# A two-layer hybrid encoder step in split fp32: squares of norms written to PSUM, adaLN reductions and two down tiles in another order

## The chip, the cores and the metric

The kernel runs on one core of a Trainium2 chip. The metric is the time of one execution on the device, in microseconds; lower is better. Before the change the median of three runs is 2359.96 us (2359.71 to 2361.61). The names used below: TensorE (PE) multiplies matrices, VectorE (DVE) and ScalarE (ACT) work element by element, GpSimd (POOL) too, and SyncE (SP) starts most DMAs.

## The reference, cut to what matters

Two groups of tokens share the weights: 512 prompt tokens and 32 sample tokens, 544 columns in all. Each of two layers has a half-step feed-forward block, a mixing block and a second half-step feed-forward block. Each block stands between two RMS norms, and each has a shift, a scale and a gate that come from a conditioning vector (adaLN).

```python
def rmsnorm(x, g):
    xf = x.astype(F32)
    r = lax.rsqrt(jnp.mean(xf * xf, axis=-1, keepdims=True) + EPS)
    return (xf * r).astype(x.dtype) * g

def swiglu(h, wg, wu, wd):
    return (jax.nn.silu(h @ wg) * (h @ wu)) @ wd
...
        mod = (jax.nn.silu(c) @ lp["w_mod"] + lp["b_mod"]).reshape(b_, N_SUB, 3, D_MODEL)
        shift, scale, gate = mod[:, :, 0, None], mod[:, :, 1, None], mod[:, :, 2, None]

        def pre(x_, j):
            return rmsnorm(x_, lp["norm_pre"][j]) * (1.0 + scale[:, j]) + shift[:, j]

        def post(x_, y_, j, w):
            return x_ + w * gate[:, j] * rmsnorm(y_, lp["norm_post"][j])

        y = swiglu(pre(x, 0), lp["ffn_w_gate"][0], lp["ffn_w_up"][0], lp["ffn_w_down"][0])
        x = post(x, y, 0, 0.5)
        y, st = token_mix(pre(x, 1), lp, prev, ssd_block)
        x = post(x, y, 1, 1.0)
        y = swiglu(pre(x, 2), lp["ffn_w_gate"][1], lp["ffn_w_up"][1], lp["ffn_w_down"][1])
        x = post(x, y, 2, 0.5)
```

D_MODEL is 1024 and D_FF is 2816. The adaLN vectors are a product of a vector of 1024 with a matrix of 1024 x 9216 in each layer.

## The kernel before, in words

The model's rows lie on partitions in 8 blocks of 128 (KD), and the tokens in two chunks c = 0 and 1 of 272 columns (CA). The whole trunk keeps fp32: a weight tile is loaded to `raw`, ScalarE copies it to a rounded `hi`, GpSimd subtracts to get `lo` (`wload`), and activations are split in the same way into `hh` and `hl`. `gemm` therefore does three matmuls for each block k (lines 276 to 278): hi by high, hi by low, lo by high.

**Feed-forward block** (`ffn`). The 22 blocks of D_FF are worked in three parts, 0 to 8, 8 to 15 and 15 to 22 (`THIRDS`). Within a part, `up(f, c, W)` makes a gate and an up product of 24 matmuls each, `g` and `u`, then Silu on ScalarE, the product on VectorE (line 421), its rounded copy on ScalarE (line 422) and the remainder on VectorE (line 423). After the gate/up tiles of a part come its down tiles, for m = 0 to 7 chunk 0 and then chunk 1, each over the 7 or 8 blocks of that part; VectorE copies the result to `Y` (line 466) or adds it (line 468). In the last part each finished `Y[m]` also goes into the sum of squares of the norm that follows (`accs[c].add(y)`).

**Norms.** An `Acc` sums squares: the first one is written to the sum itself, and for each other one `sq` (line 285) has ScalarE write the square to one of two `sq` buffers in SBUF (line 287), and VectorE, or for the blocks k in PACC GpSimd, adds it (line 321). Then `rstd` multiplies the sum by a matrix of ones on TensorE (line 296), which adds over partitions, and `finish` takes the root by Ln and Exp. `chain` returns the list of these steps for one chunk: the norm behind a block (`yacc`), `post_k` for each of 8 blocks (X is updated, lines 363 and 365, and its square goes into the next norm's sum, `acc`), the next norm and `pre_k`, which writes `hh` (line 334) and `hl` (line 335) for the next block. `weave` puts a chain's steps between the units of TensorE's work: chunk 0's chain beside the down tiles of chunk 1 in the last part, chunk 1's chain beside the first five gate/up tiles of the next block. The out-projection of the mixing block (`full`, `rest`) has the same sums.

**PSUM.** `gps6` hands out banks in turn: three `g`, two `pv` and one `tp`; while steps are woven in, three `g` and the `tp`, because the steps use the two `pv` banks for their own products (`t` in `post_k` and `pre_k`).

**adaLN.** Layer 0's first vectors are made ahead; all others come from a `Fill`: one job is a DMA of 256 KB of the adaLN weights (`mw`, three buffers, on SyncE's queue beside the weight tiles) and two VectorE reductions (line 177, `junk`), one for each token group, each followed by a short read of its sum. `fill.step(us, tail)` first issues the reductions of the jobs loaded so far, behind the instruction `tail`, and then loads so many more that all jobs would be spread over FILL_US. There is a step behind each gate/up tile and behind each down tile that isn't in the last part. Layer 0's first feed-forward block has 112 jobs, its second 96, layer 1's first 48, its second none.

What sets the order: TensorE's order is the order in which the code calls `gemm`; the instructions of VectorE and ScalarE are placed by the framework's scheduler, which holds those given with `tc.issue_after` behind the instruction named. DMAs of weights stand on one queue, and a DMA whose buffer isn't free yet holds those behind it.

Of the kernel before, what the change touches and what calls it, by code (L numbers as in the profile page):

```python
# [10 lines left out]
F32 = mybir.dt.float32  # L11
# [3 lines left out]
ALU = mybir.AluOpType  # L15
# [5 lines left out]
KD = 8  # L21
# [3 lines left out]
CA = 272  # L25
NF = 22

NHEAD = 5
FILL_US = 290

NPART = 4

# [35 lines left out]
def trunk_kernel(ctx: ExitStack, tc: tile.TileContext, a):  # L68
# [16 lines left out]
    X = [slot(f"x{k}") for k in range(KD)]  # L85
# [196 lines left out]
    SEG = (((0, CA, 0),), ((CA, SP, 0), (SP, T, 1)))  # L282


    def sq(ap):
        q = tp_.tile([128, CA], F32, tag="sq", bufs=2, name="sq")
        S.activation(q, ap, AF.Square)
        return q

# [21 lines left out]
    class Acc:  # L311
# [1 line left out]
            self.a = None  # L313
            self.tag = tag

        def add(self, ap, eng=None):
            if self.a is None:
                self.a = tp_.tile([128, CA], F32, tag=self.tag, bufs=2, name=self.tag)
                S.activation(self.a, ap, AF.Square)
            else:  # L320
                (eng or V).tensor_tensor(self.a, self.a, sq(ap), ALU.add)  # L321


    def pre_k(l, j, c, r, ks):
# [20 lines left out]
    def chain(l, j, c, Y, acc, nxt, free):  # L345
        st = {}
        xacc, pacc = Acc("acc"), Acc("acc")

        def first():
            st["r"] = rstd([acc.a], 1.0, False, bool(nxt) or c == 0)  # L350

        def post_k(k):
            if c and not nxt:
                t = tmp()
                e = G if k in FIN else V
                e.tensor_tensor(t, Y[k][:, CS[c]], st["r"], ALU.mult)
                e.tensor_tensor(X[k][:, CS[c]], X[k][:, CS[c]], t, ALU.add)
                SY.dma_start(a["o_y"][:, k, CS[c]], X[k][:, CS[c]])
                return
            t = ppv()[:, :CA]  # L360
            for (c0, c1, tok) in SEG[c]:
                o0 = c0 - c * CA
                V.scalar_tensor_tensor(t[:, o0:o0 + c1 - c0], Y[k][:, c0:c1], gpc[l][:, j, k, tok:tok + 1],
                                       st["r"][:, o0:o0 + c1 - c0], ALU.mult, ALU.mult)
            V.tensor_tensor(X[k][:, CS[c]], X[k][:, CS[c]], t, ALU.add)
            if nxt:
                if k in PACC:
                    pacc.add(X[k][:, CS[c]], G)
                else:
                    xacc.add(X[k][:, CS[c]])  # L370
            else:
                SY.dma_start(a["o_y"][:, k, CS[c]], X[k][:, CS[c]])
            if free:
                done(Y[k])

        def second():
            st["r"] = rstd([t.a for t in (xacc, pacc) if t.a is not None], 1.0, c == 1 and nxt[1] != 1, True)

        ops = [first] + [lambda k=k: post_k(k) for k in range(KD)]
        if nxt:  # L380
            ops += [second] + [lambda k=k: pre_k(*nxt, c, st["r"], [k]) for k in range(KD)]
        return ops
# [14 lines left out]
    def ffn(l, i, fill, pend, nxt, W0=(), first=(), behind=None):  # L397
# [3 lines left out]
        for ti, (f0, f1) in enumerate(THIRDS):  # L401
# [29 lines left out]
            if f == 0:  # L431
# [16 lines left out]
                    tail = up(f, 1, Ws[f] if n < 3 else load(f))  # L448
                    fill.step(5.6, tail)
                f = NHEAD  # L450
            while f < f1:
                W = load(f)
                fill.step(5.6, up(f, 0, W))
                fill.step(5.6, up(f, 1, W))
                f += 1
            nk = f1 - f0
            last = ti == 2
            if ti == 0:
# [2 lines left out]
            def down(m, c, W):  # L461
                ps = gps6()
                gemm(ps, W, range(nk), act, c)
                y = Y[m][:, CS[c]]
                if ti == 0:
                    tail = V.tensor_copy(y, ps[:, :CA])
                else:
                    tail = V.tensor_tensor(y, y, ps[:, :CA], ALU.add)
                if last:
                    accs[c].add(y)  # L470
                    if c and not nxt:
                        post_scale(l, j, m, y)
                else:
                    fill.step(0.35 * nk, tail)
# [2 lines left out]
                return wload(a["wd"][l, i, m][:, f0:f1, :], nk * 128, 2 if last else 1)  # L477

            if not last:
                for m in range(KD):  # L480
                    W = wdl(m)
                    down(m, 0, W)
                    down(m, 1, W)
            else:
                fill.flush()
                lnexp()
                Ws = []
                for m in range(KD):
                    Ws.append(wdl(m))
                    down(m, 0, Ws[m])  # L490
                units = []
                for n in range(KD):
                    m = (n + 2) % KD
                    units.append(lambda n=n, m=m: down(m, 1, Ws[m] if n < 6 else wdl(m)))
                weave(units, chain(l, j, 0, Y, accs[0], nxt, False), CUT_DN)
# [33 lines left out]
    def mix(l, pend, nxt):  # L529
# [551 lines left out]
        def full(m, c, W):  # L1081
            ps = gps6()
            gemm(ps, W, range(7), HX, c, stop=False)
            gemm(ps, W2, [m], HX[7:], c, start=False)
            S.activation(Y[m][:, CS[c]], ps[:, :CA], AF.Copy)
            accs[c].add(ps[:, :CA])

        def rest(m):
            ps = gps6()
            gemm(ps, W2, [m], HX[7:], 0)  # L1090
            y = Y[m][:, CS[0]]
            V.tensor_tensor(y, y, ps[:, :CA], ALU.add)
            accs[0].add(y)

        def wo(m):
            return wload(a["wo1"][l, m], 7 * 128, 2)
# [194 lines left out]
```

## Time and profile before

| what | value |
| --- | --- |
| median of three runs | 2359.96 us (2359.71 to 2361.61) |
| the profiled execution's own time | 2355.58 us |
| span of its trace | 2353.8 us |
| mean granted clock of TensorE | 0.977 |
| TensorE busy | 2224.8 us, 95% of the span |
| VectorE busy | 1465.6 us, 62% |
| ScalarE busy | 892.7 us, 38% |
| GpSimd busy | 1031.2 us, 44% |

All durations that follow come from the one profiled execution, whose time is 4.4 us below the median. The span is the time from the first to the last instruction of the trace. A row that names a line tells the line of the kernel before, and in the helpers `gemm`, `sq` and `Acc.add` one line serves many places; they are told apart by the names of the tiles and by the time. In a timeline row the bracket at the end holds the time for which the engine stood idle before the instruction, and what ended that.

### The profile page before, as it was taken

How to read it: one execution, taken by the hardware profiler on the slowest of the kernel's cores; microseconds unless marked ns; L12 is line 12 of the kernel's file. 1: busy time of each engine (PE TensorE's matmuls, PEld its weight loads, DVE VectorE, ACT ScalarE, POOL GpSimd, SP SyncE). 2: the span in 40 equal slices, each digit the busy share in tenths (PEclk: the TensorE clock that was granted, in tenths of full speed). 3: DMA queues.
4: the chain of work that ended last, by engine and by line, in shares of the span. 5: the costliest groups of instructions: out<-in, count | busy, mean ns of one | idle time of the engine just before them, and what ended most of it. 6: DMA issues, size and time to landing. Idle time of an engine off the chain costs nothing.

```text
span 2353.8 us, 44051 instructions
## 1 busy us (share of the span) xinstructions
PE 2224.8 (95%) x17554; PEld 2163.4 (92%) x17554; DVE 1465.6 (62%) x3281; ACT 892.7 (38%) x1796; POOL 1031.2 (44%) x689
## 2 busy tenths in 40 slices
PE   6999999988899899999989999999789999999997
PEld 5989999988888899999989999998788799999997
DVE  5798999687766779687575544447876754111114
ACT  4322222445555631222264122235555554322223
POOL 3544344553434554344355434434643444533432
PEclk9999999998999999999999999999899999999999
DMA  7454555322222345555434444332232222322222
GB/s 274 157 175 166 171 187 170 110 66 78 94 74 74 108 157 185 158 177 162 128 108 130 143 125 133 119 91 70 95 94 71 94 87 90 117 90 80 91 84 70
DMA packets 104017, 285.62 MB, mean 121 GB/s; under 512 B 12001, under 2 KB 14689, under 8 KB 103809
## 3 DMA queue, kind: packets, MB, share of 16 engines
q1 hardware_dynamic: 102146, 277.72, 36.9%
q0 software_dynamic: 1664, 5.07, 0.6%
q8 instruction: 138, 2.26, 0.4%
q14 instruction: 69, 0.57, 0.1%
HBM read 275.45 MB, written 7.30 MB: 120 GB/s over the span
## 4 chain that ended last, share of the span: by engine, by line
PE 70%; DVE 15%; issue 5%; DMA 4%; ACT 3%; POOL 3%; SPq 0%; POOLq 0%; DVEq 0%; ACTq 0%
PE g L277 12%; PE g L276 12%; PE g L278 12%; PE pv L277 6%; PE pv L278 6%; PE pv L276 6%; PE tp L276 3%; PE tp L277 3%; PE tp L278 3%; DVE junk L177 3%; DMA raw<-in_wgu 3%; POOL lo L266 2%; DVE u L564 1%; DVE acc L321 1%; PE pv L957 1%
## 5 line engine op out<-in xcount | busy, mean ns | idle before, releaser
L266 POOL TENSOR_TENSOR lo<-raw,hi 128x1024 fp32r<-128x1024 f32 (+4 forms) x498 | 918.7, 1856 | 1154.1 <-ACT hi L262 996.9
L277 PE MATMUL g<-hl,hi 128*128 128x272 f32 (+1 forms) x2402 | 699.5, 292 | 7.3 <-DVE hl L335 4.2
L276 PE MATMUL g<-hh,hi 128*128 128x272 f32 x2402 | 700.3, 293 | 6.4 <-ACT hh L334 4.9
L278 PE MATMUL g<-hh,lo 128*128 128x272 f32 (+1 forms) x2402 | 699.3, 292 | 0.0
L262 ACT ACTIVATE hi<-raw 128x1024 fp32r<-128x1024 f32 (+3 forms) x454 | 360.2, 810 | 662.4 <-PE g L277 241.0
L277 PEld LDWEIGHTS g<-hl,hi 128*128 128x128 f32 (+1 forms) x2402 | 457.3, 191 | 10.4 <-DVE hl L335 5.3
L276 PEld LDWEIGHTS g<-hh,hi 128*128 128x128 f32 x2402 | 456.5, 190 | 9.9 <-ACT hh L334 6.6
L278 PEld LDWEIGHTS g<-hh,lo 128*128 128x128 f32 (+1 forms) x2402 | 455.9, 190 | 0.7
L177 DVE CUSTOM_DVE_ANT_0 junk<-mw,csb,modr 128x512 bf16<-128x512 f32 x256 | 310.5, 1213 | 6.8 <-DMA mw<-in_wmod 1.0
L177 DVE CUSTOM_DVE_ANT_0 junk<-mw,csb 128x512 bf16<-128x512 f32 x256 | 275.3, 1075 | 7.0 <-DMA mw<-in_wmod 1.6
L278 PE MATMUL pv<-hh,lo 128*128 128x272 f32 (+1 forms) x916 | 264.0, 288 | 2.5 <-POOL lo L266 2.5
L276 PE MATMUL pv<-hh,hi 128*128 128x272 f32 (+1 forms) x916 | 264.1, 288 | 0.6 <-DVE hl L335 0.6
L277 PE MATMUL pv<-hl,hi 128*128 128x272 f32 (+1 forms) x916 | 264.4, 289 | 0.0
L276 PE MATMUL g<-u,hi 128*128 128x272 f32 x732 | 211.9, 290 | 6.7 <-ACT u L422 6.7
L277 PE MATMUL g<-u,hi 128*128 128x272 f32 x732 | 211.6, 289 | 0.2
L278 PE MATMUL g<-u,lo 128*128 128x272 f32 x732 | 211.0, 288 | 0.0
L421 DVE TENSOR_TENSOR g<-sg,g 128x272 f32<-128x272 f32 x123 | 54.5, 443 | 211.2 <-PE g L278 203.0
L278 PEld LDWEIGHTS pv<-hh,lo 128*128 128x128 f32 (+1 forms) x916 | 171.8, 188 | 2.9 <-POOL lo L266 2.9
L276 PEld LDWEIGHTS pv<-hh,hi 128*128 128x128 f32 (+1 forms) x916 | 172.2, 188 | 1.0 <-DVE hl L335 0.8
L277 PEld LDWEIGHTS pv<-hl,hi 128*128 128x128 f32 (+1 forms) x916 | 171.9, 188 | 0.0
L276 PE MATMUL tp<-hh,hi 128*128 128x272 f32 x554 | 162.9, 294 | 1.7 <-ACT hh L334 1.7
L277 PE MATMUL tp<-hl,hi 128*128 128x272 f32 x554 | 161.6, 292 | 0.0
(342 smaller groups left out, 3978.5 us busy)
## 6 DMA issues: line engine op xcount, KB each, us to landing
raw<-in_wgu SPq DMA_DIRECT2D x192, 512.0 KB, 3.6
mw<-in_wmod SPq DMA_DIRECT2D x256, 256.0 KB, 3.1
raw<-in_wd SPq DMA_DIRECT2D x72, 448.0 KB, 3.5
raw<-in_win SPq DMA_DIRECT2D x48, 512.0 KB, 3.5
raw<-in_wd SPq DMA_DIRECT2D x32, 512.0 KB, 3.7
raw<-in_wo SPq DMA_DIRECT2D x22, 448.0 KB, 3.2
u<-in_wmod SPq DMA_DIRECT2D x32, 256.0 KB, 5.3
kc<-in_kc SPq DMA_DIRECT2D x8, 512.0 KB, 4.5
```

Source lines behind the costliest of these rows:

```text
L177: V.tensor_tensor_reduce(junk, u[:, 0:512], csb[:, tok, 512 * b:512 * b + 512], 1.0, m if b else 0.0, ALU.mult, ALU.add, m)
L262: S.activation(R(hi[:, h]), raw[:, h], AF.Copy)
L266: G.tensor_tensor(R(lo[:, h]), raw[:, h], hi[:, h], ALU.subtract)
L276: PE.matmul(ps[:width, :CA], wh, R(xh[:, sl]), start=start and i == 0, stop=False)
L277: PE.matmul(ps[:width, :CA], wh, R(xl[:, sl]), start=False, stop=False)
L278: PE.matmul(ps[:width, :CA], wl, R(xh[:, sl]), start=False, stop=stop and i == n - 1)
L321: (eng or V).tensor_tensor(self.a, self.a, sq(ap), ALU.add)
L421: V.tensor_tensor(p, t, p, ALU.mult)
L564: V.scalar_tensor_tensor(o[:, 0:547], xp[:, kk:kk + 547], vl[:, w0 + kk:w0 + kk + 1], o[:, 0:547], ALU.mult, ALU.add)
L957: ins = PE.matmul(pv[64 * hh:64 * hh + 64, w0:w], vk[:, 128 * jb + 64 * hh:128 * jb + 64 * hh + 64], PT[hh][:, 128 * jb:128 * jb + 128], s ...
```

## The change

Four things change.

- `sq` takes an optional place for the square, and `Acc.add` hands it on. Three callers give one: the down tiles of the last part and the out-projection give the PSUM bank of the tile itself, whose content has just been copied or added into `Y`; `post_k` gives its product bank `t` for the blocks that aren't in PACC. Of those k = 3 is the first of its sum and has no add, so k = 5, 6 and 7 are left.
- FILL_US falls from 290 to 260, so a step loads more jobs.
- The last gate/up tile of each part has no `fill.step`, for either chunk.
- In the parts that aren't the last, the first two down weights are loaded together, and their tiles are worked in the order (m, c) = (0, 0), (1, 0), (0, 1), (1, 1).

```diff
--- before.py
+++ after.py
@@ -26,7 +26,7 @@
 NF = 22
 
 NHEAD = 5
-FILL_US = 290
+FILL_US = 260
 
 NPART = 4
 
@@ -282,8 +282,9 @@
     SEG = (((0, CA, 0),), ((CA, SP, 0), (SP, T, 1)))
 
 
-    def sq(ap):
-        q = tp_.tile([128, CA], F32, tag="sq", bufs=2, name="sq")
+    def sq(ap, q=None):
+        if q is None:
+            q = tp_.tile([128, CA], F32, tag="sq", bufs=2, name="sq")
         S.activation(q, ap, AF.Square)
         return q
 
@@ -313,12 +314,13 @@
             self.a = None
             self.tag = tag
 
-        def add(self, ap, eng=None):
+
+        def add(self, ap, eng=None, q=None):
             if self.a is None:
                 self.a = tp_.tile([128, CA], F32, tag=self.tag, bufs=2, name=self.tag)
                 S.activation(self.a, ap, AF.Square)
             else:
-                (eng or V).tensor_tensor(self.a, self.a, sq(ap), ALU.add)
+                (eng or V).tensor_tensor(self.a, self.a, sq(ap, q), ALU.add)
 
 
     def pre_k(l, j, c, r, ks):
@@ -367,7 +369,7 @@
                 if k in PACC:
                     pacc.add(X[k][:, CS[c]], G)
                 else:
-                    xacc.add(X[k][:, CS[c]])
+                    xacc.add(X[k][:, CS[c]], None, t)
             else:
                 SY.dma_start(a["o_y"][:, k, CS[c]], X[k][:, CS[c]])
             if free:
@@ -448,11 +450,14 @@
                     tail = up(f, 1, Ws[f] if n < 3 else load(f))
                     fill.step(5.6, tail)
                 f = NHEAD
-            while f < f1:
+            while f < f1 - 1:
                 W = load(f)
                 fill.step(5.6, up(f, 0, W))
                 fill.step(5.6, up(f, 1, W))
                 f += 1
+            W = load(f)
+            up(f, 0, W)
+            up(f, 1, W)
             nk = f1 - f0
             last = ti == 2
             if ti == 0:
@@ -467,7 +472,7 @@
                 else:
                     tail = V.tensor_tensor(y, y, ps[:, :CA], ALU.add)
                 if last:
-                    accs[c].add(y)
+                    accs[c].add(y, None, ps[:, :CA])
                     if c and not nxt:
                         post_scale(l, j, m, y)
                 else:
@@ -477,7 +482,11 @@
                 return wload(a["wd"][l, i, m][:, f0:f1, :], nk * 128, 2 if last else 1)
 
             if not last:
-                for m in range(KD):
+
+                Ws = [wdl(0), wdl(1)]
+                for m, c in ((0, 0), (1, 0), (0, 1), (1, 1)):
+                    down(m, c, Ws[m])
+                for m in range(2, KD):
                     W = wdl(m)
                     down(m, 0, W)
                     down(m, 1, W)
@@ -1083,14 +1092,14 @@
             gemm(ps, W, range(7), HX, c, stop=False)
             gemm(ps, W2, [m], HX[7:], c, start=False)
             S.activation(Y[m][:, CS[c]], ps[:, :CA], AF.Copy)
-            accs[c].add(ps[:, :CA])
+            accs[c].add(ps[:, :CA], None, ps[:, :CA])
 
         def rest(m):
             ps = gps6()
             gemm(ps, W2, [m], HX[7:], 0)
             y = Y[m][:, CS[0]]
             V.tensor_tensor(y, y, ps[:, :CA], ALU.add)
-            accs[0].add(y)
+            accs[0].add(y, None, ps[:, :CA])
 
         def wo(m):
             return wload(a["wo1"][l, m], 7 * 128, 2)
```

Two places show how this moves instructions. The first is VectorE at the end of part 0 of layer 0's first feed-forward block. The rows with `sg` are the products of the last gate/up tile, of chunk 0 (first) and of chunk 1; a row with `mw` is the first of the two adaLN reductions of a job (the second and the short reads are left out); a COPY is a down tile's result. Before:

```order
L421 TENSOR_TENSOR pv_1569<-sg_1594,pv_1569 128x272
L423 TENSOR_TENSOR u6_643<-pv_1569,u5_642 128x272
L177 ISA junk_121,modr0_145<-mw_1528,csb_117,modr0_145 128x512
...
L177 ISA junk_121,modr0_145<-mw_1530,csb_117 128x512
...
L421 TENSOR_TENSOR g_1632<-sg_1657,g_1632 128x272
L423 TENSOR_TENSOR u6_643<-g_1632,u5_642 128x272
L177 ISA junk_121,modr0_145<-mw_1603,csb_117,modr0_145 128x512
...
L466 COPY u7_1670<-g_1684 128x272
```

And after the change:

```order
L177 ISA junk_121,modr0_145<-mw_1469,csb_117 128x512
...
L177 ISA junk_121,modr0_145<-mw_1471,csb_117,modr0_145 128x512
...
L423 TENSOR_TENSOR pv_1575<-sg_1600,pv_1575 128x272
L425 TENSOR_TENSOR u6_643<-pv_1575,u5_642 128x272
L423 TENSOR_TENSOR g_1630<-sg_1655,g_1630 128x272
L425 TENSOR_TENSOR u6_643<-g_1630,u5_642 128x272
L471 COPY u7_1660<-g_1680 128x272
L177 ISA junk_121,modr0_145<-mw_1532,csb_117 128x512
...
L471 COPY u8_1661<-g_1714 128x272
```

The two jobs between the two chunks, four reductions, are gone; those that still come ahead of the down results all stand ahead of chunk 0's product, and the next ones stand behind the first down result.

The second place is ScalarE at the start of layer 0's second feed-forward block, where the chain of chunk 1 is woven into the first gate/up tiles. Rows with `x4` to `x7` are the squares of the next norm, `hi` rows are weight copies that wait for a DMA, and `sg` and `u` belong to a gate/up tile. Before:

```order
L287 ACTIVATE sq_9320<-x4_86 128x272
L265 ACTIVATE hi_9528<-raw_9526 128x1024
L287 ACTIVATE sq_9327<-x5_87 128x272
L420 ACTIVATE sg_9406<-g_9342 128x272
L265 ACTIVATE hi_9534<-raw_9532 128x1024
L287 ACTIVATE sq_9371<-x6_88 128x272
L287 ACTIVATE sq_9378<-x7_89 128x272
L422 ACTIVATE u16_9136<-g_9381 128x272
L291 ACT_TABLE_LOAD
```

And after the change:

```order
L321 ACTIVATE acc_9247<-x3_85 128x272
L422 ACTIVATE sg_9274<-tp_9211 128x272
L288 ACTIVATE sq_9283<-x4_86 128x272
L288 ACTIVATE pv_9286<-x5_87 128x272
L288 ACTIVATE pv_9329<-x6_88 128x272
L265 ACTIVATE hi_9488<-raw_9486 128x1024
L424 ACTIVATE u1_9097<-g_9249 128x272
L265 ACTIVATE hi_9494<-raw_9492 128x1024
L422 ACTIVATE sg_9366<-g_9304 128x272
L288 ACTIVATE pv_9335<-x7_89 128x272
```

The squares of `x5` to `x7` now go to `pv` banks; those of `x5` and `x6` stand ahead of both weight copies, and only that of `x7` stands behind the second.

## Rows read from the trace of the kernel before

**Rows 1.** The page, part 1: busy us of an engine (share of the span) and instructions.

```profile
PE 2224.8 (95%) x17554; PEld 2163.4 (92%) x17554; DVE 1465.6 (62%) x3281; ACT 892.7 (38%) x1796; POOL 1031.2 (44%) x689
```

**Rows 2.** Waits of TensorE, whole span: waiter <- ender: us, times, longest.

```profile
PE sc L296 <- DVE acc L321: 20.5, 9, 5.0
...
PE g L276 <- ACT u L422: 6.7, 3, 4.6
PE sc L296 <- DVE yacc L321: 6.7, 3, 2.6
```

**Rows 3.** Groups by shape, VectorE: count, busy us, mean ns, idle before, enders.

```profile
L177 DVE CUSTOM_DVE_ANT_0 junk<-mw,csb 128x512 bf16<-128x512 f32 x256 | 275.3, 1075 | 7.0 <-DMA mw<-in_wmod 1.6
...
L321 DVE TENSOR_TENSOR yacc<-yacc,sq 128x272 f32<-128x272 f32 x84 | 49.6, 590 | 56.8 <-ACT sq L287 56.2
...
L321 DVE TENSOR_TENSOR acc<-acc,sq 128x272 f32<-128x272 f32 x41 | 36.2, 884 | 14.8 <-ACT sq L287 13.7
L468 DVE TENSOR_TENSOR u<-u,g 128x272 f32<-128x272 f32 x68 | 29.4, 433 | 43.7 <-PE g L278 43.7
```

**Rows 4.** Timeline, VectorE, 774 to 811 us: start, us, instruction, [idle before].

```profile
777.04 0.44 DVE L321 TENSOR_TENSOR acc<-acc,sq 128x272 f32<-128x272 f32 x1
...
781.20 2.19 DVE L321 TENSOR_TENSOR yacc<-yacc,sq 128x272 f32<-128x272 f32 x1 [0.62 <-ACT sq L287]
...
806.24 2.91 DVE L321 TENSOR_TENSOR acc<-acc,sq 128x272 f32<-128x272 f32 x2 [0.61 <-ACT sq L287]
```

**Rows 5.** Timeline, GpSimd, 799 to 813 us.

```profile
805.97 2.34 POOL L266 TENSOR_TENSOR lo<-raw,hi 128x1024 fp32r<-128x1024 f32 x1 [1.62 <-ACT hi L265]
```

**Rows 6.** Timeline, ScalarE, 799 to 811 us.

```profile
804.83 1.06 ACT L265 ACTIVATE hi<-raw 128x1024 fp32r<-128x1024 f32 x1 [2.36 <-DMA raw<-in_wgu]
805.80 0.73 ACT L287 ACTIVATE sq<-x 128x272 f32<-128x272 f32 x2
```

**Rows 7.** Timeline, TensorE: the norm sums after the five stalls, layer 0.

```profile
461.83 0.73 PE L296 MATMUL sc<-yacc,ones 128*128 128x272 f32 x2 [2.61 <-DVE yacc L321]
...
777.53 0.96 PE L296 MATMUL sc<-acc,ones 128*128 128x272 f32 x3 [1.71 <-DVE acc L321]
...
809.21 2.18 PE L296 MATMUL sc<-acc,ones 128*128 128x272 f32 x4 [5.00 <-DVE acc L321]
...
1192.44 0.95 PE L296 MATMUL sc<-acc,ones 128*128 128x272 f32 x3 [2.46 <-DVE acc L321]
...
1222.82 1.28 PE L296 MATMUL sc<-acc,ones 128*128 128x272 f32 x2 [3.02 <-DVE acc L321]
```

**Rows 8.** Groups by shape, ScalarE: the squares.

```profile
L287 ACT ACTIVATE sq<-x 128x272 f32<-128x272 f32 x67 | 28.1, 425 | 17.6 <-DVE x L365 9.1 <-POOL acc L321 4.5 <-DVE acc L321 3.5
...
L287 ACT ACTIVATE sq<-g 128x272 f32<-128x272 f32 x16 | 6.3, 393 | 0.5 <-DVE yacc L321 0.5
```

**Rows 9.** Stretches of granted clock 0.50 behind stalls: their sum (eight stretches).

```profile
sum 37.55, PE 32.14 PEld 30.55 DVE 26.78 ACT 20.08 POOL 6.69; mean PE 4.02 PEld 3.82 DVE 3.35 ACT 2.51 POOL 0.84
```

**Rows 10.** Stretches, layer 0's first FFN: us, busy and instructions of each engine, PEclk.

```profile
232.00:420.00 188.00, 184.99 (x1460) 184.57 (x1460) 173.20 (x329) 47.16 (x83) 82.64 (x40) 0.99 0.53 171
```

**Rows 11.** Timeline, VectorE, end of part 0 of that FFN.

```profile
142.40 0.69 DVE L177 CUSTOM_DVE_ANT_0 junk<-mw,csb 128x512 bf16<-128x512 f32 x1
...
143.01 0.44 DVE L421 TENSOR_TENSOR pv<-sg,pv 128x272 f32<-128x272 f32 x1
...
147.91 2.70 DVE L177 CUSTOM_DVE_ANT_0 junk<-mw,csb 128x512 bf16<-128x512 f32 x1
...
151.27 0.44 DVE L421 TENSOR_TENSOR g<-sg,g 128x272 f32<-128x272 f32 x1
```

**Rows 12.** Timeline, TensorE: the first down tiles of parts 0 and 1.

```profile
143.94 0.39 PE L276 MATMUL g<-u,hi 128*128 128x272 f32 x1 [0.39 <-ACT u L422]
...
152.19 0.59 PE L276 MATMUL g<-u,hi 128*128 128x272 f32 x1 [4.63 <-ACT u L422]
...
289.44 0.39 PE L276 MATMUL pv<-u,hi 128*128 128x272 f32 x1 [2.92 <-ACT u L422]
```

## The prediction

> **What bounds the kernel now.** I read the busy shares first: TensorE works 95% of the span, 2224.8 us [rows 1]. So a change can gain only where TensorE stands still, and I went on to the table of what it waits for. Of its waits the change touches two kinds [rows 2]: the ones matmul that sums the squares of a norm (line 296) waits 20.5 us for `acc` and 6.7 us for `yacc`, each written by the VectorE add of line 321; and the first down tiles wait for the last gate/up product (line 422), 6.7 us in three places and 2.9 us in one that the order of PSUM banks lists under another name. These 37 us are the whole stake, with the clock behind them (below).
>
> The groups by shape tell why the add is late. With both inputs in SBUF it takes 0.44 us when free [rows 4], but the 41 adds into `acc` have a mean of 884 ns and the 84 into `yacc` 590 ns; `u<-u,g`, which has the same size and one operand in PSUM, has a mean of 433 ns over 68 [rows 3], which a single one blocked for 2 us would have lifted by 29 ns. The timeline at 804 us shows what the long ones share: two adds from 806.24 take 2.91 us, so the first some 2.4 [rows 4], and beside it GpSimd's weight split runs from 805.97 for 2.34 us [rows 5]. ScalarE is the other half of that stall: a weight copy there waits 2.36 us for its DMA, and the two squares stand behind it, at 805.80 [rows 6]. TensorE starts the sum at 809.21, after 5.00 us [rows 7].
>
> **The change: squares in PSUM.** All 84 adds into `yacc` (down tiles of the last part, out-projection), and three of eight in each next norm (`acc`: k = 5, 6, 7), get their square from a PSUM bank that is there anyway. No instruction is added. The square itself costs ScalarE no more (425 ns to SBUF from SBUF, 393 ns when it reads PSUM [rows 8]; writing PSUM I bound by 390 to 430 ns, below the noise of the sum). [...] I take 433 ns, the nearest row, since `u<-u,g` has exactly the new operands (one SBUF, one PSUM, SBUF out) and runs beside the same weight splits.
>
> [...] The rows have 0.44 us for the free SBUF add [rows 4] and 433 ns with a PSUM operand [rows 3]: no price for PSUM. [...]
>
> Stall by stall, with what the new order of ScalarE adds (squares no longer wait for one of two `sq` buffers, so some move ahead of a weight copy that waits for its DMA):
> - 804 us, layer 0, start of the second FFN, and its twin in layer 1: two squares go ahead of the copy that starts at 804.83, one stays behind it. Copy to 805.9, square 0.4, add 0.44, write-out: the sum starts about 807.3 in place of 809.21 [rows 6, 7]. 1.9 us twice: 3.8.
> - 777 us and twin: the last squares come directly behind the unit before; the stall of 1.71 us [rows 7] goes. 3.4.
> - 781 us and twin: a blocked `yacc` add of 2.19 us [rows 4] holds back a `hl` that TensorE waits for next; 1.0 us each: 2.0.
> - 462 us and twin in layer 1: the 2.61 us stall [rows 7] ends with a square that waits behind a weight copy; it moves ahead. What is late next is `hh`, so I take 2.1 of it: 4.2.
> - 1192 us and 1222 us (once each; layer 1's second FFN has no next norm): of 2.46 and 3.02 us [rows 7] the excess of the blocked adds goes, 1.0 and 1.6: 2.6.
>
> Together −16 us. No wait for a weight split stands behind these stalls, so what TensorE gains is passed on.
>
> **Clock.** [...] The shortest transition stall (6.7 less 4.63 and 0.39, 1.7 us [rows 2, 12]) had such a stretch behind it and the 2.46 us at 1192 had none [rows 7], so length alone doesn't tell. Bounds 0 and 11.9; I take 3, since the stalls that are only cut to 1 to 3 us may keep theirs.
>
> **The fill.** In layer 0's first FFN VectorE is nearly full with the adaLN reductions (line 177): 173.2 of 188 us [rows 10]. One takes 0.69 us free, 2.70 blocked by a weight split, 1.08 in the mean [rows 3, 11]. FILL_US 260 brings more of them per tile, and those that stood behind the last tile now come after it: nothing stands between the two chunks, but all the earlier ones stand ahead of both. At the end of part 0 that is, counted in VectorE's order from the start of the block, 36 ahead of chunk 0's product in place of 34, and 36 in place of 38 ahead of chunk 1's. Now the products start at 143.01 and 151.27, and TensorE stands still 0.39 us for the first and 4.63 us for the second [rows 11, 12]. After the change chunk 0's comes two reductions later (one free, one blocked: about 146.7, with 0.9 us to the result 147.6); TensorE needs that at 143.55, and the two chunk-0 tiles then cover chunk 1: a stall of 4.1 at most, 2.9 with both free, for 5.0, −1.5. At the end of part 1 chunk 0's product stands where chunk 1's was. Its tile is needed 2.6 us earlier (21 matmuls of 0.125) and it is spared the 0.9 us of the other chunk: 2.92 + 2.6 − 0.9 = 4.6 us [rows 12], +1.7. At the end of part 2 the same gives a first stall of 0 to 3.3, I take 1. At part 0 of layer 0's second FFN it is 1.7 + 3.0 − 0.9 = 3.8, +2.1. Sum +3 (from −4 to +7). Elsewhere VectorE has slack of 2 us or more per tile and nothing moves.
>
> **Held banks.** A bank now stays taken until the add has read it, 1 to 2 us longer; woven tiles rotate over four, and with 1460 matmuls in 188 us [rows 10] 24 of them take 3.1 us, a round 12. The next product in a `pv` bank also waits for the add two before. I put +1 us (0 to +3).
>
> **Sum**: −16 − 3 + 3 + 1 = −15 us against the profiled execution's 2355.6: 2340.6. The median of the runs shown is 4.4 higher, which gives **2345**.
>
> **Rivals.**
> 1. The stalls only change their ender. Order decides them: the weight copy that waits for its DMA ends the sum at 804 whatever the add costs, `hh` takes over at 462 us, or a bank that is held too long. That the adds stay blocked, since `acc` is still in SBUF, would do the same. For: a wait is put to the last of several. Against: the 433 ns of the same operands [rows 3]. Then half of the first term is left, −8, no clock, fill +3, banks +1: −4, 2356 (2352 to 2364). Chance 0.20.
> 2. Larger gain: the transitions lose their stalls as well, because chunk 0's tiles cover chunk 1 and the blocked reductions fall between tiles. For: chunk 1's product is the one that both big stalls waited for [rows 11, 12]. Against: VectorE is full, so a backlog is worked off nowhere. Up to −5 and 3 to 4 of clock in place of +3, −26 in all: 2334. Chance 0.10.
> 3. On the other side: the backlog decides. All of it stands ahead of chunk 0 at four transitions; if two more reductions at each are blocked (2.7 in place of 0.7 [rows 11]), each stall grows by 4: +16, with 5 us of half clock behind them. Then −16 + 3 + 16 + 5 + 1 = +9, 2369. It decides once the four transitions cost over 18 us more, 4.5 each. Against: the count ahead grows by two at the most, and part of it falls beside no split. Chance 0.08.
>
> **Chances and range.** Forecast 0.62 (2338 to 2352), rivals 0.20, 0.10, 0.08. Within 0.2% is 4.7 us, about what a measurement of this kernel can tell from no change. Faster by more: forecast, larger gain, and 0.08 of rival 1: 0.80. Same 0.12, slower 0.08. The range 2333 to 2360 leaves out rival 3, the end of rival 1 and a little below.
>
> **What would show it.** Adds with a PSUM square near 433 ns, none over 0.5 us. TensorE's wait for `acc` at about 10 in place of 20.5, for `yacc` about 2.5 (of which 1.5 is the serial end). Line 422's wait: about the same in sum, moved from part 0 to part 1. It is wrong if the adds stay long, if the norm waits come back under `sq`, `hi` or a bank, or if the waits at the transitions grow past 15 us.

## The result, and the profile after

The change takes the median from 2360.78 us (four runs) to 2332.98 us (four runs, 2331.8 to 2334.81). The ratio is 0.9884, with a 95% interval of 0.9868 to 0.9899: 27.8 us, 1.2%, faster. The prediction was 2345, so the direction and the place hold, but the gain is nearly twice the 15 us that the sum gave, and the time lies at the very lower end of the range of 2333 to 2360.

| | before | after |
| --- | --- | --- |
| median of the runs compared | 2360.78 us | 2332.98 us |
| the profiled execution's own time | 2355.58 us | 2333.70 us |
| span of its trace | 2353.8 us | 2331.1 us |
| TensorE busy | 2224.8 us | 2219.9 us |
| span less TensorE busy | 129.0 us | 111.2 us |
| mean granted clock | 0.977 | 0.981 |

The two traces differ by 22.7 us, the medians by 27.8. The other 5 us are no mechanism of the change: the profiled execution of before was 5.2 us faster than its median, the one of after 0.7 us slower than its own. In the trace 17.8 of the 22.7 us are time in which TensorE no longer stands still, and 4.9 us are busy time that it no longer needs. By an estimate 3.1 of these are the clock: without the start and the end of the kernel, TensorE's busy time in stretches of granted clock 0.50 falls from 64.4 to 57.4 us, and in both traces two matmuls of 272 columns start 125 ns apart at granted clock 1.00 and 227 ns apart at 0.50 (medians), so 0.45 of that difference is saved.

Part 1 of the page of after [rows 1]:

```profile
PE 2219.9 (95%) x17554; PEld 2161.6 (93%) x17554; DVE 1426.0 (61%) x3281; ACT 892.5 (38%) x1800; POOL 1022.1 (44%) x689
```

What TensorE waits for, after (waiter, ender: us, times, longest) [rows 2]:

```profile
PE sc L297 <- DVE acc L323: 6.9, 4, 2.2
PE g L276 <- ACT hh L336: 6.7, 7, 1.9
PE g L276 <- ACT u L424: 6.4, 2, 4.4
...
PE tp L276 <- ACT hh L336: 4.0, 2, 2.0
PE tp L276 <- ACT u L424: 3.3, 1, 3.3
...
PE g L277 <- DVE hl L337: 3.0, 1, 3.0
...
PE pv L276 <- ACT u L424: 1.8, 1, 1.8
...
PE sc L297 <- DVE yacc L323: 1.4, 1, 1.4
```

The wait for `acc` falls from 20.5 to 6.9 us, the one for `yacc` from 6.7 to 1.4, which is the serial end of the kernel. The waits for the last gate/up product (line 424, the old 422) are 6.4, 3.3 and 1.8 us, 11.5 in place of 9.6. Waits for `hh` have grown to 6.7 and 4.0 us. The adds by shape, VectorE [rows 3]:

```profile
L323 DVE TENSOR_TENSOR yacc<-yacc,g 128x272 f32<-128x272 f32 x54 | 23.5, 436 | 43.7 <-ACT g L288 42.8
...
L323 DVE TENSOR_TENSOR acc<-acc,pv 128x272 f32<-128x272 f32 x30 | 13.1, 436 | 12.4 <-ACT pv L288 10.9 <-POOL acc L323 0.8
...
L323 DVE TENSOR_TENSOR acc<-acc,sq 128x272 f32<-128x272 f32 x11 | 5.7, 519 | 5.3 <-ACT sq L288 4.8
```

Every add that reads its square from PSUM has a mean of 435 or 436 ns, where `acc` had 884 and `yacc` 590. The eleven adds left with a square in SBUF (the start, and the mixing block) still have 519. The timelines of the two traces show why: of the 34 adds of before that took over 0.6 us, 33 began while a weight split of line 266 ran on GpSimd, and every one of them ends 0.30 us behind the end of that split. In after 31 adds with a square in PSUM ran wholly inside such a split, and none took over 441 ns.

How far the trace of after is ahead of the one of before at the same norm sum, from the start of the row at line 296 or 297 in each, shows where the 22.7 us come from:

| norm sum (place) | before | after | ahead by |
| --- | --- | --- | --- |
| layer 0, end of first FFN (`yacc`) | 461.83 | 461.41 | 0.4 |
| mixing block, mid (`acc`) | 581.11 | 581.69 | −0.6 |
| out-projection (`acc`) | 777.53 | 774.25 | 3.3 |
| second FFN, start (`acc`) | 809.21 | 803.53 | 5.7 |
| second FFN, end (`acc`) | 1192.44 | 1184.44 | 8.0 |
| layer 1, first FFN, start (`acc`) | 1222.82 | 1213.69 | 9.1 |
| layer 1, first FFN, end (`yacc`) | 1612.35 | 1597.55 | 14.8 |
| layer 1, second FFN, start (`acc`) | 1957.85 | 1936.94 | 20.9 |
| last sum of the kernel | 2341.86 | 2319.14 | 22.7 |

(At 581 us the start misleads: in before the last two matmuls of this sum waited another 0.78 us, in after none did.)

The place at 804 us of before is the clearest. First VectorE, then GpSimd, ScalarE and TensorE of after in the same stretch (start, us, instruction, [idle before]):

```profile
803.04 0.44 DVE L323 TENSOR_TENSOR acc<-acc,pv 128x272 f32<-128x272 f32 x1 [2.19 <-ACT pv L288]
```

```profile
802.51 2.35 POOL L266 TENSOR_TENSOR lo<-raw,hi 128x1024 fp32r<-128x1024 f32 x1 [0.59 <-ACT hi L265]
```

```profile
801.37 1.06 ACT L265 ACTIVATE hi<-raw 128x1024 fp32r<-128x1024 f32 x1 [1.63 <-DMA raw<-in_wgu]
802.34 0.38 ACT L422 ACTIVATE sg<-g 128x272 f32<-128x272 f32 x1
802.61 0.39 ACT L288 ACTIVATE pv<-x 128x272 f32<-128x272 f32 x1
```

```profile
803.53 1.18 PE L297 MATMUL sc<-acc,ones 128*128 128x272 f32 x4 [1.97 <-DVE acc L323]
```

The add of 0.44 us now runs entirely beside a weight split of 2.35 us, where it took some 2.4 us before [rows 4, 5]. What is left of the stall, 1.97 of 5.00 us, is ScalarE: the copy that waits for its DMA until 801.37, then Silu, then the one square that stands behind them. At 462 us one wait took another's place. ScalarE there, then TensorE:

```profile
462.71 1.15 ACT L265 ACTIVATE hi<-raw 128x512 fp32r<-128x512 f32 x2 [2.36 <-DMA raw<-in_win]
463.77 0.47 ACT L336 ACTIVATE hh<-pv,modr 128x272 fp32r<-128x272 f32 x1
```

```profile
464.29 0.34 PE L276 MATMUL g<-hh,hi 128*64 128x272 f32 x1 [1.89 <-ACT hh L336]
```

The square of `yacc` now stands ahead of the two weight copies, and the sum waits for nothing; but the `hh` that TensorE wants next stands behind them, and TensorE waits 1.89 us for it.

### The profile page after: what moved, and what is told of

It reads as the page before. It is cut to its first block, busy times and chain, and to the rows that moved or that the text cites. A ratio compares the mean times of both kernels' runs of the same rounds, so it can differ in the third digit from the quotient of the medians.

```text
span 2331.1 us, 44016 instructions
## 1 busy us (share of the span) xinstructions
PE 2219.9 (95%) x17554; PEld 2161.6 (93%) x17554; DVE 1426.0 (61%) x3281; ACT 892.5 (38%) x1800; POOL 1022.1 (44%) x689
## 4 chain that ended last, share of the span: by engine, by line
PE 70%; DVE 14%; issue 5%; DMA 5%; ACT 3%; POOL 3%; SPq 0%; DVEq 0%; ACTq 0%; POOLq 0%
PE g L278 12%; PE g L277 12%; PE g L276 12%; PE pv L277 6%; PE pv L278 6%; PE pv L276 6%; DVE junk L177 4%; DMA raw<-in_wgu 4%; PE tp L276 3%; PE tp L277 3%; PE tp L278 3%; POOL lo L266 2%; DVE u L573 1%; PE pv L966 1%; DMA mw<-in_wmod 1%
## 5 line engine op out<-in xcount | busy, mean ns | idle before, releaser
L266 POOL TENSOR_TENSOR lo<-raw,hi 128x1024 fp32r<-128x1024 f32 (+4 forms) x498 | 909.3, 1837 | 1136.2 <-ACT hi L262 984.6
L276 PE MATMUL g<-hh,hi 128*128 128x272 f32 (+1 forms) x2402 | 701.2, 293 | 6.8 <-ACT hh L336 6.7
L276 PEld LDWEIGHTS g<-hh,hi 128*128 128x128 f32 (+1 forms) x2402 | 457.8, 191 | 10.3 <-ACT hh L336 8.9
L177 DVE CUSTOM_DVE_ANT_0 junk<-mw,csb,modr 128x512 bf16<-128x512 f32 x256 | 300.6, 1174 | 9.0 <-DMA mw<-in_wmod 2.9
```

Of the source, the lines that this page charges most:

```text
L177: V.tensor_tensor_reduce(junk, u[:, 0:512], csb[:, tok, 512 * b:512 * b + 512], 1.0, m if b else 0.0, ALU.mult, ALU.add, m)
L266: G.tensor_tensor(R(lo[:, h]), raw[:, h], hi[:, h], ALU.subtract)
L276: PE.matmul(ps[:width, :CA], wh, R(xh[:, sl]), start=start and i == 0, stop=False)
```

## The experiments

Five theories were told apart. A: the blocked adds hold the norm sums, and the change frees them. B: the new order at the ends of the parts carries half of the gain. C: the stalls only change their ender (rival 1 of the prediction). D: not the adds but ScalarE's order and the two `sq` buffers held the sums. F: `acc` and `yacc` aren't two separate gains. E, G, H and I belong to single runs and are told in what was expected of them. All ratios are against runs of the kernel before on the same chip.

**e1: the squares alone.** The change with its scheduling taken back:

```diff
-FILL_US = 260
+FILL_US = 290
...
-            while f < f1 - 1:
+            while f < f1:
...
-            W = load(f)
-            up(f, 0, W)
-            up(f, 1, W)
...
-                for m, c in ((0, 0), (1, 0), (0, 1), (1, 1)):
-                    down(m, c, Ws[m])
-                for m in range(2, KD):
+                for m in range(KD):
```

> The squares go to PSUM as in the change; FILL_US 290, the steps behind the last gate/up tiles and the order of the down tiles stay as before. Theory A (the norm sums carry the gain, and the half-clock stretches behind them go with the stalls): 2360.8 - 16 of stalls - 8 to 10 of clock = 2335, between 2332 and 2339; TensorE's wait for acc falls from 20.5 to about 7 us, the waits at the ends of parts 0 and 1 of layer 0's first FFN stay 4.6 and 2.9 us. Rival B (the other order at the ends of the parts carries half of it): 2345 or more, the rest being in e2. Rival C (the stalls change their ender): above 2350.

Measured: 2333.11 us, ratio 0.9876 (0.9859 to 0.9892). The waits of TensorE:

```profile
PE g L276 <- ACT u L424: 7.7, 3, 4.6
PE g L276 <- ACT hh L336: 7.2, 8, 2.1
PE sc L297 <- DVE acc L323: 6.9, 4, 2.5
...
PE pv L276 <- ACT u L424: 3.0, 1, 3.0
...
PE sc L297 <- DVE yacc L323: 1.4, 1, 1.4
```

This is the whole gain of the change, so A holds, and B and C fall here. The waits for the sums are those of after, the waits for the products at the parts' ends (7.7 and 3.0) those of before and a little more.

**e2: the scheduling alone.** The change with its three callers of `add` as before:

```diff
-                    accs[c].add(y, None, ps[:, :CA])
+                    accs[c].add(y)
...
-                    xacc.add(X[k][:, CS[c]], None, t)
+                    xacc.add(X[k][:, CS[c]])
```

(and the same in the out-projection).

> FILL_US 260, no reductions behind a part's last gate/up tile and the new order of the first two down tiles; squares stay in SBUF. Theory A: +2 to +4 us at the four transitions together (-1 at the end of part 0, -3 at part 1, +5 to +6 at part 2 with its half clock, 0 at the second FFN), so 2361 to 2365, no gain that can be told from none. Rival B: 2350 or less.

Measured: 2355.22 us beside 2359.80, ratio 0.9983 (0.9970 to 0.9996); its trace has a span of 2354.0, 0.2 us longer than that of before.

```profile
PE sc L297 <- DVE acc L323: 20.9, 10, 5.1
...
PE sc L297 <- DVE yacc L323: 6.8, 3, 2.7
...
PE g L276 <- ACT u L424: 5.0, 1, 5.0
...
PE pv L276 <- ACT u L424: 1.8, 1, 1.8
...
PE tp L276 <- ACT u L424: 1.7, 1, 1.7
```

The stalls at the parts' ends are 5.0, 1.8 and 1.7 us, 8.5 together where before has 9.6, and none is left in the second FFN. The gain is small, between 1 and 7 us by the interval, where A had expected 2 to 4 us of loss (2361 to 2365): that part of A was wrong. Added to squares that give the whole of it alone (e1 and the change are 0.1 us apart) the scheduling brings nothing that shows. B falls here too.

**e3: the order without the free adds.** Of all squares only that of k = 5 goes to PSUM, the rest is the kernel before:

```diff
-                    xacc.add(X[k][:, CS[c]])
+                    xacc.add(X[k][:, CS[c]], None, t if k == 5 else None)
```

> As before, but of the squares only that of k = 5 in the next norm's sum goes to PSUM; k = 6 and 7 and all of yacc stay in SBUF. This gives ScalarE's order of the change at the second FFN's start (only the square of k = 7 behind the second weight copy) without taking the last adds off the blocked path. Theory A (the blocked adds set the end): the 5.0 us stall at 804 us falls by 1 us at most, and the time by 2 to 6: 2355 to 2359. Rival D (the two sq buffers and the order of ScalarE are what held the sum): the 5.0 us stall falls to about 2 as in the change, and the time by 10 or more: 2350 or less.

Measured: 2357.06 us beside 2359.80, ratio 0.9982 (0.9973 to 0.9992). The last add, the split beside it and the sum in this run (VectorE, GpSimd, TensorE):

```profile
803.29 2.36 DVE L323 TENSOR_TENSOR acc<-acc,sq 128x272 f32<-128x272 f32 x1 [1.07 <-ACT sq L288]
```

```profile
803.02 2.34 POOL L266 TENSOR_TENSOR lo<-raw,hi 128x1024 fp32r<-128x1024 f32 x1 [1.73 <-ACT hi L265]
```

```profile
805.71 1.62 PE L297 MATMUL sc<-acc,ones 128*128 128x272 f32 x3 [4.48 <-DVE acc L323]
```

ScalarE's order is that of the change here, one square behind the second weight copy. The stall is 4.48 us all the same, because the last add, with both inputs in SBUF, takes 2.36 us beside the split of 2.34 us; the change's add in the same place takes 0.44. So D falls at this place. Of the 3.0 us that the change saves here, 0.5 is order and 1.9 the add; the other 0.6 is mostly the second weight copy, which in this run starts 0.66 us behind the moment TensorE runs dry and in the change 0.19 us ahead of it. e3 doesn't test D for `yacc`, whose squares and order it leaves as before (6.8 us of waits).

**e4 and e5: the two kinds of sum apart.** From e1, e4 takes the PSUM squares out of `accs` and e5 out of `xacc`:

```diff
# e4
-                    accs[c].add(y, None, ps[:, :CA])
+                    accs[c].add(y)
# e5
-                    xacc.add(X[k][:, CS[c]], None, t)
+                    xacc.add(X[k][:, CS[c]])
```

> Squares to PSUM only in the next norm's sum (k = 5, 6, 7); yacc's squares and all scheduling as before. Theory A (each sum is held by its own blocked adds, and the two kinds add up): the wait for acc falls from 20.5 to about 7 us, the wait for yacc stays 6.7; with the clock 2342 to 2347. Rival F (one of the two kinds is hidden behind the other, so either alone gives little or one alone gives all): outside 2338 to 2351.

> Squares to PSUM only in yacc (down tiles of the last part, out-projection); the next norm's sum and all scheduling as before. Theory A: the wait for yacc falls from 6.7 to about 1.4 us, the wait for acc stays near 20; 2351 to 2356, and with the kernel that moves only acc it adds up to the 27 us of both within 5. Rival F: 2345 or less, or no gain at all.

Measured: e4 2344.84 us, ratio 0.9934 (0.9920 to 0.9948); e5 2346.15 us, ratio 0.9940 (0.9921 to 0.9960), with single runs from 2341.6 to 2352.6. The waits in e4, then in e5:

```profile
PE sc L297 <- DVE acc L323: 7.3, 6, 2.3
PE sc L297 <- DVE yacc L323: 6.8, 3, 2.7
PE g L277 <- DVE hl L337: 6.5, 3, 2.9
```

```profile
PE sc L297 <- DVE acc L323: 13.8, 4, 4.0
...
PE sc L297 <- DVE yacc L323: 4.7, 3, 1.7
```

e4 is what A said. e5 isn't, in two ways. With only `yacc` freed the wait for `acc` falls too, from 20.5 to 13.8 us. Half of that is at 777 us and its twin, where `yacc`'s blocked adds stood ahead of `acc`'s on VectorE and the stall is gone with either alone; 2.2 us are at 804 us and its twin, where the last add is still blocked (2.37 us), but only one square stands behind the second copy, and this copy starts 0.14 us ahead of the moment TensorE runs dry. And the wait for `yacc` falls only to 4.7 us. ScalarE and TensorE of e5 at the place of 462 us show the rest of it:

```profile
461.64 0.63 ACT L265 ACTIVATE hi<-raw 128x512 fp32r<-128x512 f32 x1 [2.24 <-DMA raw<-in_win]
462.18 0.38 ACT L288 ACTIVATE g<-u 128x272 f32<-128x272 f32 x1
```

```profile
463.09 0.73 PE L297 MATMUL sc<-yacc,ones 128*128 128x272 f32 x2 [1.62 <-DVE yacc L323]
```

The add is free here (0.44 us), but its square still stands behind a copy that waits for its DMA, as before the change. So the free add takes 1.0 of the 2.61 us, and the other 1.6 go only in e1 and the change, where the square has moved ahead of the copies: here D is right for the larger part. No run has that order with the squares in SBUF, so what the order is worth by itself isn't shown.

The two gains, 15.4 and 14.1 us, make 29.5 where both together make 27; with single runs of e5 that differ by 11 us this isn't clear of the spread, and that each holds a part of the other rests on the waits. F is right in that, and wrong in that neither alone gives all.

**e6: reductions back behind the last tile of part 2.**

```diff
             nk = f1 - f0
             last = ti == 2
+            W = load(f)
+            if last:
+                fill.step(5.6, up(f, 0, W))
+                fill.step(5.6, up(f, 1, W))
+            else:
+                up(f, 0, W)
+                up(f, 1, W)
```

(in place of the change's three lines ahead of these)

> The change, but behind the last gate/up tile of part 2 the steps are kept, as before the change. Theory A: the reductions that the change puts ahead of chunk 0's last product there go behind it, so the new stall of 3.3 us at 412 us and the half clock behind it go, 5 us in all: 2328, between 2326 and 2330. Rival E (the higher rate of FILL_US 260 made that stall): it stays, 2333.

Measured: 2329.72 us, ratio 0.9861 (0.9841 to 0.9880). The new stall of 3.29 us that the change has at 412 us is gone from the trace, as A said: TensorE's matmuls start some 125 ns apart there, from 411.75 to 415.89 us. No row of e6 shows what became of the 3.41 us of granted clock 0.50 that the change has behind it, from 417.11. In the times the 3.3 us to the change aren't clear of the spread.

**e7 to e10: the rate of the reductions.** All have e6's edit. e7 sets FILL_US 278; e8 weighs tiles differently on top of it; e9 goes further that way (4.5, 0.55, FILL_US 284); e10 is e8 with the down tiles in the order of before.

```diff
# e8
-FILL_US = 260
+FILL_US = 278
...
-                fill.step(5.6, up(f, 0, W))
+                fill.step(5.0, up(f, 0, W))
...
-                    fill.step(0.35 * nk, tail)
+                    fill.step(0.45 * nk, tail)
```

> The change with the steps kept behind part 2's last gate/up tile, and FILL_US 278 in place of 260. At the end of part 0 as many reductions (36) stand ahead of chunk 0's product, at the end of part 1 126 in place of 132. Theory A: the stall at part 0 stays 4 to 5 us, the one at part 1 (3.0 us) goes with its half clock, 4 us less than with FILL_US 260: 2326 against 2329.7. Rival G (VectorE's backlog is set by the splits that block it and not by the count): no difference, 2329 to 2331.

> As the one with FILL_US 278, but a gate/up tile counts 5.0 in place of 5.6 and a down tile 0.45 in place of 0.35 for each block, so the reductions move from the gate/up tiles to the down tiles: 32 in place of 36 ahead of the product at the end of part 0, 126 at part 1. Theory A: four reductions less are worth 4 us there (two free, one or two blocked), so the stall of 4.6 us falls to 1 or less, and the half clock behind it goes: 2322 to 2325. If the down tiles then stand still for a bank, 2328 or more.

> A gate/up tile counts 4.5, a down tile 0.55 for each block, FILL_US 284; all else as in the kernel with 5.0 and 0.45 (2318.2 us). Ahead of the product at the end of part 0 stand 28 reductions in place of 32, at the end of part 1 126 as before, but more of them come early, beside the down tiles. Theory A: the stall at part 1 (2.0 us) depends on how far VectorE is behind there, so it goes or halves with its half clock: 2315 to 2318. Rival H (VectorE falls behind in the down tiles and TensorE waits there for a PSUM bank): 2320 or more.

> As the kernel with 5.0 and 0.45 (2318.2 us), but the first two down tiles in the order of before: (0, 0), (0, 1), then m = 1. Theory A: with no reduction between the two chunks' products chunk 1's comes 2 us after chunk 0's, and chunk 0's tile of 2.6 to 3.0 us covers that, so the order is worth nothing here: 2317 to 2320. Rival I (the order carries the gain at the parts' ends): 2321 or more, with a wait for the product of line 424 behind the first down tile.

| run | time, us | ratio (interval) | stall end of part 0 | stall end of part 1 |
| --- | --- | --- | --- | --- |
| the change | 2332.98 | 0.9884 (0.9868 to 0.9899) | 4.38 | 1.84 |
| e6 | 2329.72 | 0.9861 (0.9841 to 0.9880) | 4.66 | 3.05 |
| e7 | 2321.96 | 0.9840 (0.9823 to 0.9856) | 3.00 | none |
| e8 | 2318.19 | 0.9822 (0.9809 to 0.9835) | none | 2.02 |
| e9 | 2320.40 | 0.9838 (0.9824 to 0.9851) | none | none |
| e10 | 2321.29 | 0.9836 (0.9822 to 0.9849) | none | 2.96 |

With a lower rate the time falls by 8 us from e6 to e7, and the two stalls by 4.7 us. This speaks against G, but the intervals of e6 and e7 overlap a little. e7 and e8 came out some 4 us faster than A had said (2326, and 2322 to 2325). The count ahead of a product isn't all, either: 36 gave 4.66 us at 260 and 3.00 at 278, and 126 at the end of part 1 gave none, 2.02, none and 2.96. It seems to be how far VectorE is behind there, which the way before and the splits beside it set as well; no run isolates this. e7 also has a new wait of 3.31 us for `yacc` at 432.55, behind the first FFN's last reductions; I did not follow it up. e8 is the fastest kernel of the study, 42 us or 1.8% below before, and clear of the change (their intervals don't touch). In e9 the stall goes and another comes; TensorE's rows there are

```profile
204.96 0.36 PE L276 MATMUL pv<-hh,hi 128*128 128x272 f32 x1 [3.14 <-DVE u L475]
```

```profile
325.95 0.36 PE L276 MATMUL g<-hh,hi 128*128 128x272 f32 x1 [1.81 <-DVE modr L184]
```

The first waits 3.14 us for the VectorE add that empties a down tile's bank (line 475 of that kernel): VectorE is behind in the down tiles now, as H said. The times don't show it: the intervals of e8 and e9 overlap. e10's trace has 2.96 in place of 2.02 us at the end of part 1; its time is 3 us above e8's, at the edge of what I said for I, and the intervals overlap. Whether the order of the down tiles is worth anything stays open.

## Why the prediction was right or wrong

**The bound and the blocked adds: right.** The 433 ns taken for the new add are 435 and 436 in the trace, and none of the 114 adds is over 441 ns in the list of that line. e1 shows that the squares alone give all of the gain, and e3 that ScalarE's order at 804 us without the free adds there gives 3 us. What the squares also moved, by the scheduler, is the order at 462 us (e5); the prediction had that in its term for this place.

**The norm sums, −16: too small.** By the waits of TensorE `acc` gave 13.6 us (the terms had 3.8 + 3.4 + 2.6 = 9.8) and `yacc` 5.3 (4.2). The step that failed is the one for the place at 804 us and its twin, with 1.9 us each: 5.00 became 1.97 and 4.89 became 2.12, 2.8 to 3.0 each. The chain I wrote there (copy, square, add) is what the trace shows, 2.16 us from the copy's start to the sum. But I kept the copy at 804.83, 0.62 us behind the moment TensorE ran dry. Its DMA waits for a buffer (SyncE's issues of line 256 wait 1396.8 us for GpSimd's `lo` in after), so it moves with the work ahead, and in after the copy starts 0.19 us ahead of that moment. For 1192 us I had 1.0 and it is 1.9, for 1222 us 1.6 and it is 0.8. Another 1.6 us I hadn't counted: two sums within the mixing blocks waited 0.78 us each for a blocked add, at 582.50 and its twin, and no longer do. The term for `hl` (2.0) gave 1.2.

**`hh` as the next to be late: right, and under-sized.** I took 0.5 us off at 462 us. The waits for `hh` grew by 4.1 us (from 4.9 and 1.7 to 6.7 and 4.0). Half of that is at 483 us and its twin, 0.87 to 1.99 us each, and there it is the held bank: the product of k = 7 (476.89) waits for a `pv` bank until the add of k = 5 (476.42) has read it, so that X is ready 0.5 us later than before, and its square then stands behind an evacuation on ScalarE (478.65), for 0.5 us more. The rows, VectorE, then TensorE:

```profile
476.42 0.44 DVE L323 TENSOR_TENSOR acc<-acc,pv 128x272 f32<-128x272 f32 x1 [0.39 <-ACT pv L288]
476.89 0.47 DVE L365 SCALAR_TENSOR_TENSOR pv<-u,gpc,sc 128x240 f32<-128x240 f32 x1
477.27 0.43 DVE L323 TENSOR_TENSOR acc<-acc,pv 128x272 f32<-128x272 f32 x1
477.62 0.25 DVE L365 SCALAR_TENSOR_TENSOR pv<-u,gpc,sc 128x32 f32<-128x32 f32 x1
477.90 0.44 DVE L367 TENSOR_TENSOR x<-x,pv 128x272 f32<-128x272 f32 x1
479.38 0.44 DVE L323 TENSOR_TENSOR acc<-acc,pv 128x272 f32<-128x272 f32 x1 [1.03 <-ACT pv L288]
```

```profile
484.54 0.40 PE L276 MATMUL tp<-hh,hi 128*128 128x272 f32 x1 [1.99 <-ACT hh L336]
```

So the +1 for held banks was +2.2 of stall, with a stretch of granted clock 0.50 of 3.41 us behind the first one.

**Clock, −3: near the 3.1 us in all, too small at the norm sums.** In before the granted clock was 0.50 in eight stretches, 37.55 us, behind the stalls of the change: 23.9 us of them behind norm sums and 13.7 behind gate/up transitions. The bound of 11.9 was half of the 23.9. No run shows that half, nor the −3 itself; what the traces show is the 125 and 227 ns above, 0.45, by which the bound is an estimated 10.7. After there are five stretches, three in old places and two new ones, at 417 and 485 us [rows 9]:

```profile
sum 20.48, PE 19.41 PEld 19.21 DVE 13.30 ACT 11.90 POOL 13.78; mean PE 3.88 PEld 3.84 DVE 2.66 ACT 2.38 POOL 2.76
```

Of those behind norm sums only the one at 464 us is left, now behind the wait for `hh`. Those behind 804, 1222 and 1957 us are all gone, though stalls of 1.97, 2.23 and 2.12 us stay, while a stall of 2.02 us at 887.65 keeps one. My reason for taking only 3 of 11.9 (that cut stalls keep their stretch) failed there: the four stretches that went from behind norm sums held 17.5 us of TensorE's work, an estimated 7.9 us by the same 0.45. The new stretches, and the mixing block (below), took part of that back; all busy time together fell by 4.9 us.

**The fill, +3: the sum holds in the trace, the parts don't.** TensorE's rows at the four places, after [rows 12]:

```profile
148.53 0.60 PE L276 MATMUL g<-u,hi 128*128 128x272 f32 x1 [4.38 <-ACT u L424]
```

```profile
285.41 0.39 PE L276 MATMUL pv<-u,hi 128*128 128x272 f32 x1 [1.84 <-ACT u L424]
```

```profile
415.75 0.39 PE L276 MATMUL tp<-u,hi 128*128 128x272 f32 x1 [3.29 <-ACT u L424]
```

```profile
887.65 0.39 PE L276 MATMUL g<-u,hi 128*128 128x272 f32 x1 [2.02 <-ACT u L424]
```

Against the forecast: 4.4 for 2.9 to 4.1; 1.8 for 4.6; 3.3 for 1; 2.0 for 3.8. The larger stall did not move to part 1, as the prediction's signs had it. Its bounds at part 0 don't come out of rows 11 either: two free reductions give a stall of some 2.0 us and not 2.9, and nothing there rules out two blocked ones, some 6. At the end of part 1 I had put chunk 0's product where chunk 1's had been by its place in VectorE's order, which is right, and then at the same time, which is wrong: it came at 284.49 in place of 288.52; the six reductions right ahead of it all ran free (0.69 to 0.75 us), where two of before's four took 2.5 us. How many fall beside a weight split can also differ between executions: e6 has the same order up to there and 3.05 us. At the end of part 2 the reductions that the missing step left over were flushed ahead of chunk 0's product. e6 shows that by removing it.

**Not forecast at all: the mixing block.** Its first transposes waited 15.3 and 6.5 us (for lines 579 and 681 of before) and wait 11.7 and 5.1 after; other waits there grew by some 2 us. The change doesn't touch these lines. It comes with the squares: e3, with one of them moved, has it as well (10.3 and 5.2 us), and e2, with none, has not (15.2 and 6.7). That the scheduler orders the convolutions anew is likely, but not shown. In stalls it is worth about 3 us; but TensorE's busy time at granted clock 0.50 in the two mixing blocks grew from 32.2 to 38.0 us, an estimated 2.6 us, so it brings little in all.

**The offset.** I carried the 4.4 us between the profiled execution and the median over to the changed kernel. It has none (2333.70 against 2332.98). One execution's offset is chance: single runs of before lie between 2351.5 and 2365.5 us.

Of the 12 us by which 2345 was too high, 5 are that offset and 7 the profiled execution (7.7 by its span). Of the 7.7 about 4 are the norm sums with `hl`, 3 the stalls of the mixing block, 2 the busy time and 1 the fill, with 2 to 3 going the other way by `hh`. So the mechanism held, and most of its terms were taken too small; the 5 us of the offset are chance. The time is the one that rival 2 gave, but not by its mechanism: the transitions kept their stalls, 11.5 us. Rival 1 is seen at one place, 462 us and its twin, where the stall changed its ender. Rival 3 did not come up: it needed 16 us at the transitions, and together they grew by 1.9.

**The price of PSUM: none, as the rows of before had it.** An add of 272 columns took 436 ns with a PSUM operand in after, and a free one from SBUF 0.44 us in before [rows 4].

## What to carry to other kernels

Where a group's mean in the profile is far above its shortest row, look at what runs beside the long rows; if it is GpSimd, give one operand of the VectorE instruction a place in PSUM (here the mean of the adds into `acc` went from 884 to 436 ns). Then look at the order of the other engines again: it moves with such a change, and can hold part of the gain (462 us). A square, a product or another throwaway can go to the bank that was just read, but count who wants that bank next (the wait for `hh` at 483 us went from 0.87 to 1.99 us). And filler work should be weighed so that the engine that does it has caught up where another engine next depends on it: three such edits (e8) were worth 15 us on top of the change's 28.

## What the runs showed of the hardware that was not expected

- An add with both inputs in SBUF isn't slowed in proportion beside GpSimd's weight split; it ends 0.30 us behind it, in all 33 cases of before. The add at 803.29 of e3 ends at 805.65, the split from 803.02 at 805.36, and the change's add with one PSUM operand in the same place isn't touched at all: 0.44 us inside a split of 2.35, against 2.36 in e3.
- The lower clock behind a stall doesn't follow from its length: 2.02 us at 887.65 of after was followed by 3.41 us at granted clock 0.50, 2.23 us at 1213.69 by none. The change saved 17.8 us of stalls and 4.9 us of busy time; of the latter an estimated 3.1 are the clock.
- Single executions of one kernel differed by up to 14 us (before, 2351.5 to 2365.5 us over 19 runs), so one traced execution is good for where the time goes and not for the last 5 us of a median.
